# A hybrid SSD and attention encoder layer: z and most of the values projected with tokens on partitions, in blocks of 256 channels

## The chip, the cores and the metric

The kernel runs on one core of one Trainium2 chip. The metric is the device time of one execution in microseconds; the number given for a kernel is the median of its runs. Engines are called as in the profile: TensorE (PE, its weight loads PEld), VectorE (DVE), ScalarE (ACT), GpSimd (POOL) and SyncE (SP), whose queue issues every DMA of this kernel.

## What is computed

One encoder layer on a sequence of 1024 tokens of width 1024, in float32. The cut below leaves out the details of the two halves.

```
h   = layer_norm(x)
z, xbc, dt_f, dt_b, q, k, v, g = split(h @ w_in)       # 1024, 1536, 16, 16, 1024 x 4 channels
y_ssm  = rms_norm(ssd(conv_silu(xbc), dt_f, dt_b) * silu(z))   # forward and backward, chunks of 128
y_attn = rms_norm((softmax1 - lam * softmax2) @ v) * silu(g)   # 8 heads, v of 128 channels each
out = layer_norm(alpha * h + concat(y_ssm, y_attn) @ w_out)
```

The gate needs silu(z) with tokens on partitions, since y_ssm is kept so. The weighted sums need v with tokens (the keys) on partitions, since they are the contracted dimension. q, k, g and the convolution's inputs are used with channels on partitions.

## The kernel before, in words

**Precision.** Matrix operands are split in two parts of a reduced float32 (fp32r): a rounded part "hi" and the rest "lo". A product takes three matmuls: hi by hi, lo by hi, hi by lo.

**Projection.** The normalised input lies transposed in SBUF, channels on partitions, as 16 tiles of 128x512 each for hi and lo (`h_hi`, `h_lo`, lines 279 and 280). `Block` (line 296) is a projection of 128 output channels. The lane `fill` (line 328) computes a block in two halves of the sequence: for each half one PSUM bank, 8 steps over the input channels, three matmuls each, with the weights as the stationary operand (128x128) and 512 tokens as the moving one. That is 48 matmuls a block, and there are NB = 52 blocks. When a half is done, the block's `evac` takes the bank.

The lane `weights` (line 306) loads the weights of the next block in two parts of 256 KB into two staging tiles `wst`, and `split_w` splits each part: ScalarE rounds it into `whi`, POOL subtracts to get `wlo`. There are four places each for `whi` and `wlo`; a block of 128 channels uses two.

**z and v before.** Because a block comes out with channels on partitions, z (line 465) and v (line 921) are turned: `evac` copies the bank into an SBUF tile (`zr` or `vc`), and a lane of its own (`z_tail`, `v_tail`) transposes it in four matmuls against the identity into another bank, from where ScalarE takes silu (z) or ScalarE and VectorE split it (v). z goes to DRAM (`zd`) and is read back by the lane `gate` (line 820).

**Order of the blocks.** b, c and x of the first SSD group; z of group 0 (4 blocks); x, b and c of group 1; z of group 1 (4 blocks); then q, k, v, g for each of the 8 heads. A block may have a condition (`when`); q and k of head h, for instance, wait for the scores of head h-2, and v for its weighted sums, because two heads share the tiles in turn (`free_since`, line 883).

**Order of the instructions.** The work is written as lanes (generators), and the class `Loom` (line 47) weaves them into one order: it estimates from a table of costs when each tile will be ready and lets the lane with the lowest rank go on that would not make TensorE wait. The ranks and margins are in `LANES` (line 29); projection (`fill`) has rank 9, so it fills what the others leave. TensorE keeps this order; ScalarE, VectorE, POOL and the DMA queue are ordered by the framework's scheduler.

**Stages in time.** Up to about 105 us: input, norm, first blocks. 105 to 206 us: SSD of group 0 beside the z blocks. 206 to 289: x, b, c of group 1. 289 to 432: SSD of group 1 beside z of group 1 and q, k, v of head 0. From 432: attention, where each head has scores, exponentials, the difference of the two maps (`combine`), transposes of the map and weighted sums of the values (`values`, line 1029, 24 matmuls of 256 columns for 256 queries). From about 960 the output projection joins. Nearly every instruction is recorded with line 140, the line of the helper that issues it, so the rows are told apart by their tiles: `bk<-hh,whi` is a projection's hi by hi, `bk<-ident,zr` a transpose of z, `bk<-wh,vh` a weighted sum.

Of the kernel before, what the change touches and what calls it, by code (L numbers as in the profile page):

```python
# [18 lines left out]
S = 1024  # L19
# [3 lines left out]
NB = 52  # L23
# [4 lines left out]
# rank of each lane, and how much later than estimated it takes its inputs to be ready  # L28
# [101 lines left out]
class Engine:  # L130
    """An engine whose instructions are noted in the loom."""
# [21 lines left out]
class Pool:  # L153
    """A tile pool whose slots' reuse is noted in the loom; under are the pools whose place it takes."""
# [62 lines left out]
def hybrid_layer_kernel(  # L217
# [70 lines left out]
    def places_w():  # L288
        return [wp.tile([128, 4, 128], F32R, name=n, bufs=4) for n in ("whi", "wlo")]
# [6 lines left out]
    class Block:  # L296
        """128 projected channels; evac(half, psum) takes each half of the sequence."""

        def __init__(self, col, evac, when=None, after=None):
            self.col, self.evac, self.when, self.after = col, evac, when, after  # L300
            self.w, self.begun = [], 0
# [4 lines left out]
    def weights():  # L306
        """Loads and splits the weights of a block while the one before it is computed."""
        for n in range(NB):
# [5 lines left out]
            yield lambda: before.begun > 0  # L314
            sts = []
            for i in range(2):
                st, src = stage_w(b.col, i, wp, 2)
                yield st
                dma(st, src)
                sts.append(st)  # L320
            if not before.pair:
                yield lambda: before.begun > 1
            for st in sts:
                hi, lo = places_w()
                yield (st, hi)
                b.w.append(split_w(st, hi, lo))

    def fill():
        n = 0
        while n < NB:  # L330
# [5 lines left out]
            for b in blocks:  # L336
                if b.when is not None:
                    yield b.when
            for half in range(2):
                for b in blocks:  # L340
# [3 lines left out]
                    for k in range(KB):  # L344
# [10 lines left out]
                        if k == 0:  # L355
                            b.begun += 1
                        if b.last:
# [10 lines left out]
    # ================= embedding LayerNorm and bidirectional SSD =================  # L368
# [30 lines left out]
    def conv_block(b, when, dst_of, after):  # L399
        """Block b of x/B/C: raw projection, then convolution and SiLU into dst_of()."""  # L400
# [31 lines left out]
    def to_tokens(src, put):  # L432
        """Transposes src [128 ch, S]; put(half, psum [128 tokens, 4, 128])."""
# [31 lines left out]
    def z_block(g, j, when=None):  # L465
        def evac(half, ps):
            zr = late["sq"].tile([128, 512], F32, name="zr", bufs=2)
            A.copy(zr, ps)

            def tail():  # L470
                pt = bank((128, 4, 128))
                yield (zr, pt)
                for i in range(4):
                    transpose(pt[:, i, :], zr[:, 128 * i:128 * i + 128])
                zs = late["sq"].tile([128, 4, 128], F32, name="zs", tag="zr", bufs=2)
                A.activation(zs, pt, AF.Silu)
                dma(zd[g][4 * half:4 * half + 4, :, 128 * j:128 * j + 128].rearrange("c p n -> p c n"), zs)
                G[g].z_done += 1
            loom.add(tail(), "z_tail")
        queue.append(Block(Z0 + 512 * g + 128 * j, evac, when))  # L480

    with tc.tile_pool(name="dp", bufs=1) as dp_, tc.tile_pool(name="p0", bufs=1) as p0_:
# [45 lines left out]
        def to_channels():  # L528
            for half in range(2):
                for kk in range(0, KB, 4):  # L530
                    pts = [sbank() for _ in range(4)]
                    for js in ((0, 1, 2), (3,)):
                        for k in range(kk, kk + 4):
# [17 lines left out]
                            if half == 0 and k in (1, 3):  # L551
                                b = first[k // 2]
                                b[0].w.append(split_w(b[1], *places_w(), act=AO))
# [22 lines left out]
        def steps_lane():  # L576
            """Step sizes, decays and their sums within chunks."""
# [103 lines left out]
        for b, st in first[:2]:  # L681
            b.w.append(split_w(st, *places_w(), act=AO))
# [12 lines left out]
    def ssd(g):  # L695
# [72 lines left out]
        def maps():  # L768
            """Within-chunk maps of one head, four chunks at a time."""
# [84 lines left out]
    for j in range(4):  # L854
# [5 lines left out]
    for j in range(4):  # L860
# [453 lines left out]
```

## Time and profile before

| | us |
|---|---|
| median of 3 runs | 1239.81 |
| the runs | 1235.19 to 1240.91 |
| span of the profiled execution (its own time is not given otherwise) | 1236.1 |
| TensorE busy | 1176.0 (95%) |
| VectorE busy | 933.8 (76%) |
| ScalarE busy | 677.8 (55%) |
| POOL busy | 479.9 (39%) |

The span runs from the first to the last instruction of the profiled execution and is that execution's time as far as it is recorded. Busy time counts an instruction from start to end; matmuls overlap, so the sum of their durations is larger than the time they take, and the distance from one start to the next is what one costs. A row of the timeline gives start, duration, engine, line, operation, tiles and shape.

### The profile page before, as it was taken

How to read it: one execution, taken by the hardware profiler on the slowest of the kernel's cores; microseconds unless marked ns; L12 is line 12 of the kernel's file. 1: busy time of each engine (PE TensorE's matmuls, PEld its weight loads, DVE VectorE, ACT ScalarE, POOL GpSimd, SP SyncE). 2: the span in 40 equal slices, each digit the busy share in tenths (PEclk: the TensorE clock that was granted, in tenths of full speed). 3: DMA queues.
4: the chain of work that ended last, by engine and by line, in shares of the span. 5: the costliest groups of instructions: out<-in, count | busy, mean ns of one | idle time of the engine just before them, and what ended most of it. 6: DMA issues, size and time to landing. Idle time of an engine off the chain costs nothing. (4 is left out here: it accounts for less than half of the span.)

```text
span 1236.1 us, 16398 instructions
## 1 busy us (share of the span) xinstructions
PE 1176.0 (95%) x5881; PEld 922.4 (75%) x5881; DVE 933.8 (76%) x1334; ACT 677.8 (55%) x1181; POOL 479.9 (39%) x404
## 2 busy tenths in 40 slices
PE   5998999899899999999999999999999998999997
PEld 3787666788567777777787777877777776778885
DVE  6687888867988568788788787887878889962334
ACT  4556356734457456665755656556656687641221
POOL 7422664323654323223332333233332429541354
PEclk9999999999899999999999999999999998999999
DMA  6113335522245421012112111121111263233221
GB/s 198 32 33 112 89 112 167 178 69 65 89 118 151 132 72 49 26 44 51 26 35 52 43 44 35 34 52 35 43 28 47 81 209 107 55 123 112 78 85 60
DMA packets 107591, 98.03 MB, mean 79 GB/s; under 512 B 9364, under 2 KB 79349, under 8 KB 107509
## 3 DMA queue, kind: packets, MB, share of 16 engines
q1 hardware_dynamic: 107509, 96.98, 27.2%
q8 instruction: 46, 0.75, 0.2%
q14 instruction: 36, 0.29, 0.1%
HBM read 75.85 MB, written 16.91 MB: 75 GB/s over the span
## 5 line engine op out<-in xcount | busy, mean ns | idle before, releaser
L140 PE MATMUL bk<-hh,whi 128*128 128x512 f32 x832 | 353.2, 425 | 0.6
L140 PE MATMUL bk<-hl,whi 128*128 128x512 f32 x832 | 327.0, 393 | 3.2 <-POOL hl L140 2.8
L140 PE MATMUL bk<-hh,wlo 128*128 128x512 f32 x832 | 328.0, 394 | 0.0
L140 ACT ACTIVATE p<-p,nm 128x1024 f32<-128x1024 f32 x128 | 146.8, 1148 | 121.7 <-DVE nm L140 121.0
L140 POOL TENSOR_TENSOR wlo<-wst,whi 128x512 fp32r<-128x512 f32 x104 | 161.5, 1557 | 126.9 <-ACT whi L140 109.2
L140 POOL TENSOR_SCALAR p<-p,rs 128x1024 f32<-128x1024 f32 x56 | 64.5, 1152 | 350.4 <-DVE rs L140 287.5
L140 PEld LDWEIGHTS bk<-hh,wlo 128*128 128x128 f32 x832 | 156.6, 188 | 34.9
L140 PEld LDWEIGHTS bk<-hl,whi 128*128 128x128 f32 x832 | 157.7, 190 | 32.9 <-POOL hl L140 5.4
L140 PEld LDWEIGHTS bk<-hh,whi 128*128 128x128 f32 x832 | 157.7, 190 | 32.7 <-issue 5.8
L140 DVE CUSTOM_DVE_ANT_0 p<-sc,dist 128x1024 f32<-128x1024 f32 x128 | 151.3, 1218 | 11.6 <-PE sc L140 10.9
L140 DVE SCALAR_TENSOR_TENSOR p<-p,rs,p 128x1024 f32<-128x1024 f32 x64 | 128.4, 2007 | 22.1 <-POOL p L140 18.0
L140 DVE TENSOR_TENSOR wl<-bk,wh 128x512 fp32r<-128x512 f32 x128 | 87.0, 684 | 15.6 <-ACT wh L140 13.7
L140 ACT CAST wh<-bk 128x512 fp32r<-128x512 f32 x128 | 74.1, 580 | 43.2 <-PE bk L140 42.7
L140 ACT CAST whi<-wst 128x512 fp32r<-128x512 f32 x104 | 64.2, 620 | 46.9 <-PE bk L140 38.1
L140 PE MATMUL bk<-ident,p 128*128 128x128 f32 x512 | 79.4, 278 | 4.7 <-DVE wl L140 2.7
L140 PEld LDWEIGHTS bk<-ident,p 128*128 128x128 f32 x512 | 61.6, 142 | 29.5 <-DVE wl L140 6.2
L140 PE MATMUL bk<-wh,vh 128*128 128x256 f32 x256 | 74.6, 291 | 0.0
L140 PE MATMUL bk<-wl,vh 128*128 128x256 f32 x256 | 72.2, 282 | 0.7 <-DVE wl L140 0.7
L140 PE MATMUL sc<-kk,q 128*128 128x512 f32 x256 | 72.3, 393 | 0.0
L140 PE MATMUL bk<-wh,vl 128*128 128x256 f32 x256 | 72.0, 281 | 0.0
L140 ACT ACT_TABLE_LOAD x42 | 53.9, 1283 | 25.5 <-DVE t L140 15.7
L140 PEld LDWEIGHTS bk<-xt,t 128*128 128x128 f32 x256 | 45.8, 192 | 26.5 <-issue 15.0
(217 smaller groups left out, 2188.1 us busy)
## 6 DMA issues: line engine op xcount, KB each, us to landing
wst<-in_w_in_dram SPq DMA_DIRECT2D x104, 256.0 KB, 3.0
t<-acs_d SPq DMA_DIRECT2D x64, 256.0 KB, 3.5
ws<-in_w_out_dram SPq DMA_DIRECT2D x32, 256.0 KB, 3.1
ys<-yd SPq DMA_DIRECT2D x32, 256.0 KB, 3.0
xb<-in_x_dram SPq DMA_DIRECT2D x8, 512.0 KB, 6.2
zd<-zs SPq DMA_DIRECT2D x16, 256.0 KB, 2.5
gz<-zd SPq DMA_DIRECT2D x16, 256.0 KB, 3.3
yd<-ys SPq DMA_DIRECT2D x16, 256.0 KB, 2.8
```

The costliest lines, as they stand in the source:

```text
L140: r = f(*args, **kw)
```

## The change

z and the values of heads 1 to 6 are projected the other way round: a tile of the normalised input (128 tokens) is the stationary operand and the weights of 256 channels are the moving one, so that the result has tokens on partitions. `fill_wide` computes such a block as four PSUM banks, each with two groups of 128 tokens by 256 channels; a group is 8 steps of three matmuls with 256 columns, a block 192 matmuls. z takes 4 such blocks instead of 8, and the values of heads 1 and 2, 3 and 4, 5 and 6 take one each; NB falls from 52 to 45. Heads 0 and 7 keep the old way. silu of z and the split of v read the projection's banks directly.

A wide block's weights come in four parts of 256 input rows by 256 channels, of the same 256 KB, through the same two staging tiles, and use all four places of `whi` and `wlo`. `weights` now waits, before it takes a place, until the block that had it has been computed from it (`spent`), and it loads part i+2 after the split of part i.

The values have three places in turn instead of two (head modulo 3): place 0 in the pool `ep`, 1 and 2 in the pool `ap`, so v waits for the sums of the head three before. The wide block of heads h and h+1 waits for head h-2. The places of the third pair of value tiles are among those that the output projection's rows take later (`late_rows`). The descriptor scratch of the DMAs is set to 1024 bytes. Comments and docstrings are gone too.

```diff
-NB = 52
+NB = 45
...
-    def stage_w(col, i, pool, bufs):
-        st = pool.tile([128, 4, 128], F32, name="wst", bufs=bufs)
-        return st, w_in[512 * i:512 * i + 512, col:col + 128].rearrange("(k p) n -> p k n", p=128)
+    def stage_w(col, i, pool, bufs, n=1):
+
+        st = pool.tile([128, 4 // n, 128 * n], F32, name="wst", bufs=bufs)
+        r = 512 // n
+        return st, w_in[r * i:r * i + r, col:col + 128 * n].rearrange("(k p) c -> p k c", p=128)
...
+    def places_w(b):
+        placed.append((b, len([1 for a, _ in placed if a is b])))
+        n = b.wide
+        return [wp.tile([128, 4 // n, 128 * n], F32R, name=t, bufs=4) for t in ("whi", "wlo")]
...
+            parts = 2 * b.wide
             sts = []
...
+            for i in range(parts + 2):
+                if i >= 2:
+                    if i == 2 and not before.pair:
+                        yield lambda: before.begun > 1
+                    a, j = placed[-4] if len(placed) > 3 else (b, -1)
+                    yield lambda: a.spent > j
+                    hi, lo = places_w(b)
+                    yield (sts[i - 2], hi)
+                    b.w.append(split_w(sts[i - 2], hi, lo))
+                if i < parts:
+                    st, src = stage_w(b.col, i, wp, 2, b.wide)
+                    yield st
+                    dma(st, src)
+                    sts.append(st)
+
+    def fill_wide(b):
+        for i in range(4):
+            ps = bank((128, 2, 256))
+            loom.held.add(ps.name)
+            half = i // 2
+            yield ps
+            for t in range(2):
+                c = 128 * (2 * i + t - 4 * half)
+                c = slice(c, c + 128)
+                for k in range(KB):
+                    if len(b.w) <= k // 2:
+                        yield lambda: len(b.w) > k // 2
+                    hi, lo = b.w[k // 2]
+                    yield (hi, lo)
+                    hi, lo = hi[:, k % 2, :], lo[:, k % 2, :]
+                    T.matmul(ps[:, t, :], h_hi[half][k][:, c], hi, start=(k == 0), stop=False)
+                    T.matmul(ps[:, t, :], h_lo[half][k][:, c], hi, start=False, stop=False)
+                    T.matmul(ps[:, t, :], h_hi[half][k][:, c], lo, start=False, stop=(k == KB - 1))
+                    if k == 0 and i % 2 == 0 and t == 0:
+                        b.begun += 1
+                    if i == 3 and t == 1:
+                        b.spent = (k + 1) // 2
+            b.evac(i, ps)
+            loom.held.remove(ps.name)
...
     def z_block(g, j, when=None):
-        def evac(half, ps):
-            zr = late["sq"].tile([128, 512], F32, name="zr", bufs=2)
-            A.copy(zr, ps)
...
-        queue.append(Block(Z0 + 512 * g + 128 * j, evac, when))
+        def evac(i, ps):
+            zs = late["sq"].tile([128, 2, 256], F32, name="zs", tag="zr", bufs=2)
+            A.activation(zs, ps, AF.Silu)
+            dma(zd[g][2 * i:2 * i + 2, :, 256 * j:256 * j + 256].rearrange("c p n -> p c n"), zs)
+            G[g].z_done += 1
+        queue.append(Block(Z0 + 512 * g + 256 * j, evac, when, wide=True))
...
+    def places_v(h):
+
+        H = heads_[h]
+        pool = att["ap"] if h % 3 else ep
+        H.vh, H.vl = [pool.tile([128, NCH, 128], F32R, name=f"{n}{h % 3}") for n in ("vh", "vl")]
+
+    def proj_vv(h):
...
+            for n, H in enumerate(pair):
+                if i == 0:
+                    places_v(h + n)
+                t, c = slice(2 * i, 2 * i + 2), slice(128 * n, 128 * n + 128)
+                A.copy(H.vh[:, t, :], ps[:, :, c])
+                V.tensor_sub(H.vl[:, t, :], ps[:, :, c], H.vh[:, t, :].bitcast(F32))
+                H.v += 0.5
+        free = (lambda: state["open"]) if h == 1 else (lambda: heads_[h - 2].summed == 4)
+        queue.append(Block(V0 + 128 * h, evac, free, wide=True))
...
-        queue.append(Block(V0 + 128 * h, evac, free_since(h, "summed", 4)))
+        queue.append(Block(V0 + 128 * h, evac, None if h == 0 else lambda: heads_[h - 3].summed == 4))
...
+                ("vh2", (2, 512), 1, lambda: heads_[5].summed == 4), ("vl2", (2, 512), 1, None),
                 ("gate", (2, 512), 2, lambda: heads_[6].done == 2),
...
-    nc = _bacc.Bacc("TRN2", target_bir_lowering=False, num_devices=1)
+    nc = _bacc.Bacc("TRN2", target_bir_lowering=False, num_devices=1,
+                     dynamic_dma_scratch_size=1024)
```

## Rows read from the trace of the kernel before

**Rows 1.** Busy time by stretch: length, then busy us (count) per engine.

```profile
core 0: us, PE busy (x) PEld busy (x) DVE busy (x) ACT busy (x) POOL busy (x), PEclk, DMA share, GB/s
105.00:206.00 101.00, 93.63 (x430) 68.13 (x430) 83.97 (x108) 57.29 (x111) 53.04 (x42) 0.98 0.34 103
289.00:432.00 143.00, 131.87 (x615) 99.53 (x614) 113.68 (x150) 71.17 (x136) 67.57 (x54) 0.98 0.40 116
480.00:960.00 480.00, 478.13 (x2581) 378.32 (x2580) 388.46 (x579) 293.14 (x511) 147.39 (x108) 1.00 0.16 40
960.00:1110.00 150.00, 140.48 (x712) 111.48 (x711) 125.55 (x172) 103.89 (x174) 77.91 (x53) 0.97 0.37 116
1110.00:1236.00 126.00, 118.27 (x510) 95.55 (x509) 44.99 (x83) 22.71 (x34) 49.61 (x41) 0.98 0.27 84
```

**Rows 2.** Waits of TensorE: total us, times, longest.

```profile
PE sb L140 <- DVE H L140: 9.1, 8, 2.7
PE bk L140 <- DVE t L140: 5.9, 5, 1.5
...
PE bk L140 <- ACT vc L140: 1.5, 2, 1.0
...
PE bk L140 <- ACT zr L140: 1.0, 1, 1.0
```

**Rows 3.** TensorE's timeline: projection, then the first set of a v block.

```profile
493.81 0.39 PE L140 MATMUL bk<-hh,whi 128*128 128x512 f32 x1
...
497.69 0.39 PE L140 MATMUL bk<-hh,wlo 128*128 128x512 f32 x1
498.20 0.65 PE L140 MATMUL bk<-ident,vc 128*128 128x128 f32 x4
498.61 0.48 PE L140 MATMUL bk<-hh,whi 128*128 128x512 f32 x1
498.93 0.39 PE L140 MATMUL bk<-hl,whi 128*128 128x512 f32 x1
```

**Rows 4.** TensorE's timeline: a second set of v, and a set of z.

```profile
588.28 0.63 PE L140 MATMUL bk<-ident,vc 128*128 128x128 f32 x4
588.67 0.48 PE L140 MATMUL bk<-hh,whi 128*128 128x512 f32 x1
588.98 0.39 PE L140 MATMUL bk<-hl,whi 128*128 128x512 f32 x1
...
363.78 0.60 PE L140 MATMUL bk<-ident,zr 128*128 128x128 f32 x4
364.21 0.33 PE L140 MATMUL bk<-xt,t 128*128 128x64 f32 x2
```

**Rows 5.** Timeline: 24 matmuls of a weighted sum, and one weight load.

```profile
700.90 0.28 PE L140 MATMUL bk<-wh,vh 128*128 128x256 f32 x1
...
703.66 0.28 PE L140 MATMUL bk<-wh,vl 128*128 128x256 f32 x1
...
701.02 0.19 PEld L140 LDWEIGHTS bk<-wh,vl 128*128 128x128 f32 x1
```

**Rows 6.** Tiles zr, whi, wlo (ns min/median/max), and DMA issues (KB, us to landing).

```profile
L140 ACT COPY zr<-bk x16: 562/578/590, 118.7 to 390.2; 128x512 f32<-128x512 f32 x16
...
L140 ACT CAST whi<-wst x36: 600/618/639, 109.2 to 430.0; 128x512 fp32r<-128x512 f32 x36
L140 POOL TENSOR_TENSOR wlo<-wst,whi x36: 1267/1306/2351, 109.9 to 430.6; 128x512 fp32r<-128x512 f32 x36
...
L140 POOL TENSOR_TENSOR wlo<-wst,whi x48: 1274/1468/2290, 486.7 to 946.4; 128x512 fp32r<-128x512 f32 x48
...
wst<-in_w_in_dram SPq DMA_DIRECT2D x104, 256.0 KB, 3.0
...
ws<-in_w_out_dram SPq DMA_DIRECT2D x32, 256.0 KB, 3.1
```

**Rows 7.** One third of the projection's matmuls, 480 to 960 us and 105 to 432.

```profile
L140 PE MATMUL bk<-hh,whi 128*128 128x512 f32 x384 | 160.5, 418 | 0.6
...
L140 PE MATMUL bk<-hh,whi x278: 387/393/1414, 105.0 to 429.3; 128*128 128x512 f32 x139
```

**Rows 8.** Waits of SP's queue: total us, times, longest.

```profile
SPq L140 <- POOL wlo L140: 517.0, 95, 29.0
```

**Rows 9.** Busy time of two stretches; the granted clock stands third from the end.

```profile
120.00:160.00 40.00, 36.61 (x175) 27.00 (x174) 33.82 (x44) 18.01 (x35) 22.73 (x18) 0.96 0.29 86
...
320.00:360.00 40.00, 37.69 (x152) 26.07 (x150) 34.08 (x42) 20.82 (x42) 21.22 (x16) 0.91 0.36 101
```

More of the change, by code (lines that the diff above doesn't have):

```diff
@@ L282, in hybrid_layer_kernel @@
     h_used = [0, 0]
-    def stage_w(col, i, pool, bufs):
-        st = pool.tile([128, 4, 128], F32, name="wst", bufs=bufs)
-        return st, w_in[512 * i:512 * i + 512, col:col + 128].rearrange("(k p) n -> p k n", p=128)
-    def places_w():
-        return [wp.tile([128, 4, 128], F32R, name=n, bufs=4) for n in ("whi", "wlo")]
+    def stage_w(col, i, pool, bufs, n=1):
+        st = pool.tile([128, 4 // n, 128 * n], F32, name="wst", bufs=bufs)
+        r = 512 // n
+        return st, w_in[r * i:r * i + r, col:col + 128 * n].rearrange("(k p) c -> p k c", p=128)
+    placed = []
+    def places_w(b):
+        placed.append((b, len([1 for a, _ in placed if a is b])))
+        n = b.wide
+        return [wp.tile([128, 4 // n, 128 * n], F32R, name=t, bufs=4) for t in ("whi", "wlo")]
     def split_w(st, hi, lo, act=A):
@@ L296, in hybrid_layer_kernel, with __init__ @@
     class Block:
-        def __init__(self, col, evac, when=None, after=None):
+        def __init__(self, col, evac, when=None, after=None, wide=False):
             self.col, self.evac, self.when, self.after = col, evac, when, after
-            self.w, self.begun = [], 0
+            self.w, self.begun, self.spent = [], 0, 0
+            self.wide = 2 if wide else 1
             self.pair = self.last = False
@@ L306, in weights @@
     def weights():
-        for n in range(NB):
+        n = -1
+        while n < NB - 1:
+            n += 1
             yield lambda: len(queue) > n
@@ L314, in weights @@
             yield lambda: before.begun > 0
+            parts = 2 * b.wide
             sts = []
[L316 to L326, printed above, removed]
+            for i in range(parts + 2):
[36 more added lines that the diff above has]
+            loom.held.remove(ps.name)
     def fill():
@@ L338, in fill @@
                     yield b.when
+            if blocks[0].wide == 2:
+                yield from fill_wide(blocks[0])
+                continue
             for half in range(2):
@@ L356, in fill @@
                             b.begun += 1
+                        if half:
+                            b.spent = (k + 1) // 4
                         if b.last:
@@ L465, in z_block @@
     def z_block(g, j, when=None):
-        def evac(half, ps):
-            zr = late["sq"].tile([128, 512], F32, name="zr", bufs=2)
-            A.copy(zr, ps)
[L470 to L479, printed above, removed]
-        queue.append(Block(Z0 + 512 * g + 128 * j, evac, when))
+        def evac(i, ps):
[4 more added lines that the diff above has]
+        queue.append(Block(Z0 + 512 * g + 256 * j, evac, when, wide=True))
     with tc.tile_pool(name="dp", bufs=1) as dp_, tc.tile_pool(name="p0", bufs=1) as p0_:
@@ L681, in hybrid_layer_kernel @@
         for b, st in first[:2]:
-            b.w.append(split_w(st, *places_w(), act=AO))
+            b.w.append(split_w(st, *places_w(b), act=AO))
         first = first[2:]
@@ L852, in ssd @@
             loom.add(lane())
-    for j in range(4):
+    for j in range(2):
         z_block(0, j)
@@ L859, in hybrid_layer_kernel @@
     bc_block(1, "c", lambda: G[0].fwd == NCH)
-    for j in range(4):
+    for j in range(2):
         z_block(1, j)
@@ L919, in proj_k, with evac @@
         queue.append(Block(K0 + 128 * h, evac, free_since(h, "scored", 8)))
+    def places_v(h):
[3 more added lines that the diff above has]
+    def proj_vv(h):
+        pair = heads_[h:h + 2]
+        def evac(i, ps):
+            for n, H in enumerate(pair):
[7 more added lines that the diff above has]
+        queue.append(Block(V0 + 128 * h, evac, free, wide=True))
     def proj_v(h):
@@ L925, in evac @@
             if half == 0:
-                H.vh = H.pool().tile([128, NCH, 128], F32R, name="vh")
-                H.vl = H.pool().tile([128, NCH, 128], F32R, name="vl")
+                places_v(h)
             vc = (att["ap"] if h else late["sq"]).tile([128, 512], F32, name="vc", tag="zr", bufs=2)
@@ L956, in project_head @@
     def project_head(h):
-        for f in (proj_q, proj_k, proj_v, proj_g):
+        if h % 2 == 0 or h == 7:
+            fs = (proj_q, proj_k, proj_v, proj_g) if h in (0, 7) else (proj_q, proj_k, proj_g)
+        else:
+            fs = (proj_q, proj_k, proj_vv, proj_g)
+        for f in fs:
             f(h)
```

2 lines of the change are left out of this document (1 added, 1 removed), and 2 rows, old and new, of the table last.

## The prediction

> **What bounds the kernel now.** I read the busy time by stretch first, since the page's average mixes stages. In the attention stretch, 480 to 960 us, TensorE is busy for 478.1 of 480 us, VectorE for 388 and ScalarE for 293 [rows 1]: there every microsecond of TensorE time taken away should come off the end, and every hole put in should be added. In the two SSD stretches (105 to 206 and 289 to 432 us) TensorE is busy for 93.6 of 101 and 131.9 of 143, and VectorE for 83 and 79% of the time. Two things share the limit there: projection work, which fills the gaps, and a chain through VectorE. From 960 us on TensorE again does nearly all (140.5 of 150, 118.3 of 126). The waits of TensorE come next: little stands there at all, and most of it is the SSD's (9.1 us for the state tile H, 5.9 for the maps t), against 1.0 us for the z copies and 1.5 for the v copies [rows 2]. So I price TensorE's time first, by the distance from start to start in its timeline, because the printed durations overlap.
>
> **What goes: 112 transposes.** z loses 16 sets of four, heads 1 to 6 lose 12 sets; heads 0 and 7 keep theirs.
> A v block has two sets. Around the first, the last projection matmul starts at 497.69 and the transposes at 498.20, though a matmul takes 0.228 us to the next start (17 steps from 493.81 to 497.69) [rows 3]: 0.28 us of waiting for the copy out of PSUM. The four then hold the engine until 498.61, and the first matmul behind them takes 0.32 instead of 0.23. Start of the next regular matmul: 498.93, where without the set it would have been 498.15. The set costs 0.78 us. The second set waits for nothing: from 588.28 to 588.98, less one matmul, 0.47 us [rows 4]. Six blocks by 1.25 us: -7.5 us.
> A z set takes 0.43 us (363.78 to 364.21) and is followed by other small work, so no slow restart comes on top [rows 4]. 16 by 0.43 is 6.9 us; the wait for the copies adds 1.0 [rows 2]: -7.9 us.
>
> **What comes: twice as many matmuls of half the width.** 7 wide blocks of 192 matmuls with 256 moving columns (1344) stand in for 14 blocks of 48 with 512 (672). The same form already runs in the weighted sums of the values: 128x128 stationary, 256 columns, a fresh weight load each, 23 steps from 700.90 to 703.66 us, 0.120 us per step [rows 5]. 1344 x 0.120 = 161.3 us. The old form: 672 x 0.228 = 153.4; I take 154 since short runs elsewhere step by 0.23. So +7 us (+6 to +8), of which 3/7 in the attention stretch. Each form carries 13 to 15 ns beyond its columns at the granted full clock of 2.4 GHz, and halving the width pays that twice.
> The Trainium skill (TensorE: Matmul & The Clock Gate, section "Back-to-back issue gap") gives N/2.4 + 2.5 ns for an isolated matmul, with a fixed cost of only 2.5 ns. By that two narrow ones would cost 2.5 ns more than one wide one, 1.7 us over 672 instead of 7, and the sum would be 5 us better; the rows differ from it, and I go by them.
> Net on TensorE: -7.5 - 7.9 + 7 = -8.4 us.
>
> **ScalarE, VectorE, POOL.** 28 copies out of PSUM of 0.58 us leave ScalarE [rows 6]; SiLU of z and the splits of v stay, now straight from the projection's banks. In the attention stretch ScalarE is 61% busy, so this is worth nothing by itself; in the SSD stretches, where it feeds the chain, it may be worth something: 0 to -6 us, a third of the 18.5 us in which TensorE idles there [rows 1]. I take 0, because the waits on record name VectorE's tiles. The weight splits are as many as before (104 on ScalarE, 104 on POOL).
>
> **DMA.** The loads of weights are as many and as large (38 x 2 + 7 x 4 = 104 of 256 KB), with rows of 1 KB instead of 512 B for the wide ones. Loads of the same size with rows of 2 KB (w_out) land after 3.1 us, those of 512 B after 3.0 [rows 6]: no gain. The stores of z keep number and size. No DMA here is issued by POOL, so I cost the smaller scratch at 0: it frees SBUF for the third place of values. That place costs nothing and loosens one wait: v of heads 3 and 4 wait for head 1's sums, as v of head 3 did before.
>
> **The new wait: places for weights.** A wide block holds all four places of split weights until its last 128 tokens. The next block's first split can begin only when the first quarter of the last 24 matmuls is done, 18 x 0.120 = 2.2 us before the block's end. Cast 0.62 us on ScalarE, subtraction 1.3 to 1.5 on POOL [rows 6]: ready about at the end. Before, splits were done a block ahead.
> Wide to narrow (5 times): part 0 in time to some tenths late, part 1 done 1.1 us after the end and needed 12 x 0.228 = 2.7 after. Narrow to wide (5 times): the fourth part's place comes free with the narrow block's last matmul and its split takes 1.9 us; it is needed after 18 x 0.120 = 2.2. So 0 to 1 us each, by how long ScalarE and POOL have other work in front. Wide to wide (twice, between the z blocks): there are two staging tiles, so the load of part 2 waits for POOL's subtraction of part 0, takes 3.0 us, and its split 1.9: ready 4.7 us after the end, needed after 1.4; part 3 0.6 later still. About 4 to 4.5 us of bare projection time each.
> Bare sum: 9 for the two, up to 10 for the ten others. What covers it: projection is only 55% of the attention stretch (3 x 384 matmuls by 0.228 are 263 of 480 us) and 58% of the time from 105 to 432 us (3 x 278, 190 of 327 us) [rows 7], so the last 24 matmuls and the first of the next block are spread over twice the time, and the planner puts other lanes where weights are late. If the cover is gone, the 19 us count in full. Bounds 0 and +19; I take +3, near the lower end, as the trace shows two lanes side by side in every stretch in question. Behind the waiting casts stand the exponentials of the scores on ScalarE, behind the waiting loads the k shifts and decay rows on SP's queue. That queue already stands for 517 us in all behind POOL's subtraction [rows 8] while TensorE hardly waits for anything it brings, so I add nothing.
>
> **The sum.** -8.4 + 3 = -5.4 us: 1236.1 (the profiled span; no other time of that execution is recorded) to 1230.7. The span is 3.7 us under the median of 1239.8 and inside the runs shown (1235.2 to 1240.9), so I predict 1234.4 for the median. 0.5% is 6.2 us, about what a measurement of this kernel can tell from no change: faster means under 1233.6.
>
> **Rivals.**
> *The SSD's share is lost.* If VectorE's chain sets the end of the SSD stretches, z's transposes cost nothing today and their removal brings nothing; then only -7.5 + 3 in attention counts, with 2 us of holes: about 1237.3. For it: VectorE at 80% there, H as the longest wait. Against: TensorE at 92%, and work left over is done later anyway.
> *More than the transposes goes.* If every hand-over is covered and the chain runs freer without z copies and ring waits on ScalarE: -8.4 - 6, 1225.4. For it: 18.5 us of idle TensorE in these stretches. Against: only 1.0 us of it is put down to z.
> *Slower: weights come late.* The mechanism above, uncovered: -8.4 + 19 = +10.6, 1250.4. It decides from 8.4 us of holes on (slower at all), 14.6 for a clear loss. The place is between the two z blocks of each group, and at each wide block's ends. The clock may add to it: in the stretches 120 to 160 and 320 to 360 us, just where these blocks fall, the granted clock was 0.96 and 0.91 [rows 9], so part of them ran at the lower level of 1.2 GHz after idle patches; 9% of 40 us is 3.6 us of work lost in the second, and longer holes could cost that again.
> *The narrow form doesn't reach its pitch.* If a matmul had to wait for its own load of 0.19 us [rows 5], 1344 x 0.07 us would be 94 us more, about 1330. The rows that price it show loads of 0.19 us overlapping at 0.120 us per step, so 1%.
>
> **Chances.** Forecast 44%: holes of 0 to 6 us put it between -8.4 and -2.4, a third of it past the bound of -6.2 (16% faster, 28% the same). SSD's share lost 16%: nearly all the same. More goes 25%: nearly all faster. Late weights 14%: 11% slower, 3% the same. Pitch 1%. Together faster 0.40, same 0.46, slower 0.14. The range 1224 to 1247 leaves out the far end of the good case and the worse half of the late weights. The likeliest case alone spans 1231 to 1238.
>
> **What would show it.** Right: distances of 0.12 us between the new matmuls; no transposes of zr, and four sets of vc; the period of an attention head shorter by about 0.7 us on average, odd heads long and even ones short; holes of under 2 us at the hand-overs. Wrong: TensorE idle before the first matmuls of a wide block's successor, released by POOL's subtraction; low clock around 155 and 335 us for longer than now; a steeper pitch; or the SSD's end staying at 432 us while its TensorE time falls.

## The result, and the profile after

The changed kernel takes **1271.87 us** (median of 4 runs, 1264.21 to 1277.12), the kernel before, timed with it, 1240.36: a ratio of **1.0258**, 95% interval 1.0222 to 1.0294. It is slower by 2.6%, where 1234.4 us was predicted with a range of 1224 to 1247. The profiled execution is the shortest of the four; its span grew from 1236.1 to 1262.5 us, +26.4, and these are the microseconds that the traces can place. The other 5 of the median's 31.5 are seen only in that the mean granted clock of the four runs is 0.972 to 0.985, against 0.990 in the trace of before.

Busy time by stretch, kernel after (length, then busy us and count for each engine, granted clock, DMA share, GB/s), to be laid beside [rows 1]:

```profile
105.00:206.00 101.00, 85.84 (x538) 69.01 (x537) 87.00 (x111) 52.92 (x104) 50.39 (x39) 0.98 0.33 103
289.00:432.00 143.00, 133.42 (x789) 109.34 (x788) 110.09 (x155) 69.33 (x129) 66.47 (x53) 0.98 0.39 114
480.00:960.00 480.00, 463.65 (x2732) 382.55 (x2731) 356.66 (x566) 281.31 (x495) 141.66 (x106) 0.99 0.16 39
960.00:1110.00 150.00, 132.51 (x690) 103.82 (x689) 125.86 (x185) 100.24 (x170) 67.04 (x47) 0.97 0.31 95
1110.00:1262.00 152.00, 143.34 (x639) 116.53 (x638) 59.49 (x101) 36.88 (x59) 60.98 (x49) 0.99 0.30 93
```

TensorE's idle time (length less busy) went from 7.4 to 15.2 us in the first SSD stretch, from 11.1 to 9.6 in the second, from 1.9 to 16.3 in attention and from 9.5 to 17.5 in the stretch where the output projection joins. What ended the waits of TensorE, kernel after (total us, times, longest):

```profile
PE sb L140 <- DVE H L140: 15.2, 10, 3.7
...
PE bk L140 <- DVE osl L140: 8.9, 4, 2.7
...
PE bk L140 <- DVE wl L140: 3.6, 4, 2.2
...
PE bk L140 <- DVE vl L140: 2.3, 1, 2.3
```

Against [rows 2], H has grown by 6 us, and osl, wl and vl now stand there with 14.8. POOL's `wlo`, the late weights that the prediction feared, is not in this list. The list names only what ended a wait, though; whether projection work stood ready to fill it has to be looked up for each hole. The longest hole of attention in TensorE's timeline, kernel after:

```profile
687.64 0.28 PE L140 MATMUL bk<-whi,hh 128*128 128x256 f32 x1
...
688.96 0.28 PE L140 MATMUL bk<-wlo,hh 128*128 128x256 f32 x1
689.08 0.60 PE L140 MATMUL bk<-ident,p 128*128 128x128 f32 x4
689.91 0.49 PE L140 MATMUL bk<-osh,ones_r 128*128 128x512 f32 x1 [0.23 <-ACT osh L140]
693.10 0.51 PE L140 MATMUL bk<-osl,ones_r 128*128 128x512 f32 x1 [2.69 <-DVE osl L140]
693.44 0.40 PE L140 MATMUL bk<-hh,whi 128*128 128x512 f32 x1
```

The same time on VectorE, then on POOL:

```profile
689.09 2.28 DVE L140 SCALAR_TENSOR_TENSOR p<-p,rs,p 128x1024 f32<-128x1024 f32 x1
691.29 1.75 DVE L140 TENSOR_TENSOR osl<-osq,osh 128x512 fp32r<-128x512 f32 x1
```

```profile
690.24 2.25 POOL L140 TENSOR_TENSOR wlo<-wst,whi 128x512 fp32r<-128x512 f32 x1
```

From 687.64 to 688.96 the wide form takes 11 steps of 0.120 us, the price that was taken from [rows 5]. Then TensorE stops at a matmul of the lane `finish` (the sum of squares that closes a part of a head, `ones_r`), which the planner had put first and whose operand `osl` VectorE makes only after a difference of two maps of 2.28 us. But the projection's next block was not ready either: the low part of its first weights is done at 692.49 us, 3.2 us after the wide block's end. The hole from 859.00 to 861.68 us has the same two causes. In the other holes of attention over 0.4 us, 10.3 of the 16.3 us, the weights of the next projection matmul stood ready. This one lies within a group of a wide block:

```profile
820.88 0.28 PE L140 MATMUL bk<-wlo,hh 128*128 128x256 f32 x1
821.00 0.60 PE L140 MATMUL bk<-ident,p 128*128 128x128 f32 x4
823.85 0.47 PE L140 MATMUL bk<-osh,ones_r 128*128 128x512 f32 x1 [2.24 <-DVE wl L140]
...
824.38 0.40 PE L140 MATMUL bk<-whi,hh 128*128 128x256 f32 x1
```

```profile
812.08 1.29 POOL L140 TENSOR_TENSOR wlo<-wst,whi 128x512 fp32r<-128x512 f32 x1 [0.32 <-ACT whi L140]
```

The weights for 824.38 were split by 813.37 us, and the group's bank was open. TensorE keeps the planner's order, so a matmul placed too early stops everything behind it.

How far attention moved is read from the first score matmul of each head. Of the eight in the kernel after (duration in ns, start in us), three:

```profile
L140 PE MATMUL sc<-kk,q x1: 477/477/477, 435.1 to 435.1; 128*128 128x512 f32 x1
...
L140 PE MATMUL sc<-kk,q x1: 390/390/390, 516.4 to 516.4; 128*128 128x512 f32 x1
...
L140 PE MATMUL sc<-kk,q x1: 393/393/393, 1015.6 to 1015.6; 128*128 128x512 f32 x1
```

The heads start at 435.1, 516.4, 599.9, 675.6, 767.4, 844.2, 936.1 and 1015.6 us. Before, they start at 432.4, 509.6, 589.4, 669.2, 749.1, 828.8, 908.6 and 989.1: a cycle that repeats to 0.2 us for five heads. This splits the 26.4 us without a rest: attention begins 2.7 later, the first head takes 81.3 instead of 77.2 (+4.1), the next six together 499.2 instead of 479.5 (+19.7), and from the last head's start to the end of the span it is 246.9 instead of 247.0.

### The profile page after: what moved, and what is told of

It reads as the page before. It is cut to its first block, busy times and chain, and to the rows that moved or that the text cites. A ratio compares the mean times of both kernels' runs of the same rounds, so it can differ in the third digit from the quotient of the medians.

```text
span 1262.5 us, 17501 instructions
## 1 busy us (share of the span) xinstructions
PE 1173.2 (93%) x6441; PEld 952.7 (75%) x6441; DVE 903.8 (72%) x1346; ACT 668.0 (53%) x1166; POOL 473.1 (37%) x404
## 5 line engine op out<-in xcount | busy, mean ns | idle before, releaser
L140 PE MATMUL bk<-hh,whi 128*128 128x512 f32 x608 | 250.0, 411 | 2.5 <-ACT raw L140 2.1
L140 PE MATMUL bk<-hl,whi 128*128 128x512 f32 x608 | 239.7, 394 | 3.2 <-POOL hl L140 3.0
L140 PE MATMUL bk<-hh,wlo 128*128 128x512 f32 x608 | 240.2, 395 | 0.0
L140 PE MATMUL bk<-whi,hh 128*128 128x256 f32 x448 | 145.0, 324 | 0.0
L140 PEld LDWEIGHTS bk<-hh,whi 128*128 128x128 f32 x608 | 114.9, 189 | 28.2 <-issue 3.6
L140 PE MATMUL bk<-whi,hl 128*128 128x256 f32 x448 | 127.1, 284 | 0.0
L140 PE MATMUL bk<-wlo,hh 128*128 128x256 f32 x448 | 127.1, 284 | 0.0
L140 DVE TENSOR_TENSOR wl<-bk,wh 128x512 fp32r<-128x512 f32 x128 | 87.4, 685 | 26.4 <-ACT wh L140 24.5
L140 PEld LDWEIGHTS bk<-whi,hh 128*128 128x128 f32 x448 | 86.3, 193 | 5.7 <-issue 5.1
L140 PEld LDWEIGHTS bk<-whi,hl 128*128 128x128 f32 x448 | 86.4, 193 | 5.5 <-issue 5.1
L140 PEld LDWEIGHTS bk<-wlo,hh 128*128 128x128 f32 x448 | 85.9, 192 | 0.2 <-POOL wlo L140 0.2
L140 PEld LDWEIGHTS bk<-ident,p 128*128 128x128 f32 x512 | 60.2, 141 | 34.0 <-issue 14.2
```

The costliest lines, as they stand in the source:

```text
L140: r = f(*args, **kw)
```

## The experiments

Sixteen further kernels. **Margin** below is a number of the planner's table `LANES`: microseconds that it adds to the time at which it expects a lane's tiles to be ready. It changes no operand, no size and no count of an instruction, only the order. The **end of the plan** is the planner's own sum of estimated costs in its bookkeeping, no time of the chip. In the table, "ratio" is to the kernel before on the same chip (medians of runs on different chips are not compared, only what each has over that), "first" the start of head 0's scores, "cycle" the mean distance of the starts of heads 1 to 7, "rest" from head 7's start to the end of the span (us, profiled execution).

| kernel | median | ratio (95%) | span | first | cycle | rest |
|---|---|---|---|---|---|---|
| before | 1240.4 | 1 | 1236.1 | 432.4 | 79.9 | 247.0 |
| after | 1271.9 | 1.0258 (1.0222–1.0294) | 1262.5 | 435.1 | 83.2 | 246.9 |
| e1 z wide | 1282.2 | 1.0323 (1.0280–1.0365) | 1286.0 | 444.8 | 87.1 | 237.8 |
| e2 values wide | 1263.4 | 1.0187 (1.0157–1.0217) | 1262.0 | 434.5 | 83.9 | 246.1 |
| e3 places, scratch | 1239.3 | 1.0003 (0.9987–1.0020) | 1236.5 | 430.4 | 79.9 | 248.9 |
| e4 after, banks freed early | 1279.3 | 1.0312 (1.0282–1.0342) | 1277.3 | 441.7 | 86.7 | 235.1 |
| e5 after, values 0.2 | 1250.1 | 1.0112 (1.0088–1.0136) | 1248.5 | 442.4 | 82.1 | 233.6 |
| e6 before, values 0.2 | 1246.6 | 1.0090 (1.0067–1.0114) | 1244.0 | 435.3 | 80.3 | 251.8 |
| e7 before, values 0.8 | 1284.6 | 1.0400 (1.0374–1.0425) | 1282.3 | 431.3 | 88.4 | 237.5 |
| e8 after, values 0.2, 5 places | 1254.3 | 1.0149 (1.0115–1.0184) | 1250.6 | 440.2 | 82.3 | 239.4 |
| e9 after, values 0.3 | 1251.0 | 1.0113 (1.0085–1.0141) | 1247.1 | 436.7 | 80.6 | 246.7 |
| e10 z wide, scores 1.2 | 1254.3 | 1.0135 (1.0110–1.0161) | 1249.1 | 439.1 | 80.4 | 246.5 |
| e11 after, finish 2.2, 5 places | 1253.2 | 1.0121 (1.0098–1.0144) | 1246.6 | 436.4 | 80.7 | 249.3 |
| e12 before, combine 0.4 | 1241.9 | 1.0033 (1.0018–1.0048) | 1240.3 | 432.9 | 80.1 | 249.1 |
| e13 values wide, values 0.2 | 1249.3 | 1.0089 (1.0068–1.0111) | 1246.7 | 432.8 | 83.7 | 233.3 |
| e14 values wide, finish 2.2 | 1260.1 | 1.0180 (1.0159–1.0201) | 1259.3 | 437.5 | 83.8 | 241.9 |
| e15 z wide, group 0 only | 1246.2 | 1.0056 (1.0036–1.0075) | 1244.5 | 439.8 | 79.9 | 248.2 |
| e16 z wide, group 1 only, scores 1.2 | 1245.1 | 1.0054 (1.0037–1.0072) | 1246.9 | 436.1 | 80.5 | 246.7 |

### The parts alone, and the banks: e1 to e4

e1 keeps the wide z, e2 the wide values, e3 neither (three places for values and the small scratch alone). e4 is the changed kernel with wide values copied out of their bank at once.

```diff
e1, NB = 48:
-        if h % 2 == 0 or h == 7:
-            fs = (proj_q, proj_k, proj_v, proj_g) if h in (0, 7) else (proj_q, proj_k, proj_g)
-        else:
-            fs = (proj_q, proj_k, proj_vv, proj_g)
-        for f in fs:
+        for f in (proj_q, proj_k, proj_v, proj_g):
... (v of heads 1 and 2 waits for state["open"], since no head stands three before them)
e2: z_block and its calls as before, NB = 49
e3: both, NB = 52
e4:
+                if n == 0:
+                    vc = att["ap"].tile([128, 2, 256], F32, name="vc", tag="zr", bufs=2)
+                    A.copy(vc, ps)
-                A.copy(H.vh[:, t, :], ps[:, :, c])
-                V.tensor_sub(H.vl[:, t, :], ps[:, :, c], H.vh[:, t, :].bitcast(F32))
+                A.copy(H.vh[:, t, :], vc[:, :, c])
+                V.tensor_sub(H.vl[:, t, :], vc[:, :, c], H.vh[:, t, :].bitcast(F32))
```

> z wide, all values narrow with three places. Theory BANKS (the wide blocks of values hold the four shared PSUM banks until VectorE's subtraction, so projection stalls in attention): the attention stretch is as full as before (TensorE 478 of 480 us), only the holes between the wide z blocks stay, 1240 + 4 = 1244 us (1238 to 1250). Theory WEIGHTS (late split weights at every wide block): 4 of the 7 wide blocks are left, more than half of the loss, 1256 us (1252 to 1262).

> z narrow with transposes, values of heads 1 to 6 wide. BANKS: nearly the whole loss stays, 1263 us (1257 to 1270), with TensorE idle for 12 us or more between 480 and 960 us. WEIGHTS: 3 of 7 wide blocks, 1253 us (1248 to 1257), and the idle time stands right behind the three wide blocks.

> Nothing wide: z and values as before, but three places of values, the places' tags, late rows and small scratch of the change. BANKS and WEIGHTS: 1240 us (1236 to 1244). Rival PLACES (the third place or the scratch itself costs): over 1250 us.

> The change, but a wide block of values is copied out of PSUM by one ScalarE copy per bank and split from SBUF, so the bank is free without VectorE. BANKS: the holes of attention go (TensorE 475 of 480 us or more) and with them part of the thin tail, 1272 - 14 - 6 = 1252 us (1245 to 1257). WEIGHTS: no change, 1272 us (1267 to 1276).

e3 sits on the kernel before: the third place and the scratch cost nothing. e2 came out as the theory BANKS had it, with 16.3 us of idle TensorE between 480 and 960 us. What either theory expected of e1 and e4 fell. z alone loses 3.2%, more than the whole change, and the parts don't add (+3.2 and +1.9 against +2.6). Freeing the banks early made it slower, but e4 got another order as well (its cycle is 86.7 us), so it doesn't clear the banks. The strangest is e1: its attention has the same instructions as the kernel before, yet their cycle went from 79.9 to 87.1 us. Its busy time by stretch, columns as above:

```profile
480.00:960.00 480.00, 467.98 (x2508) 372.70 (x2507) 356.56 (x549) 285.88 (x493) 138.44 (x105) 1.00 0.16 39
960.00:1110.00 150.00, 123.72 (x600) 96.10 (x599) 115.51 (x164) 90.68 (x152) 64.18 (x46) 0.90 0.30 93
```

12 us of idle TensorE where before had 1.9, and 26 in the next stretch instead of 9.5, with the weights of the next projection matmul ready in every hole over 0.4 us up to 960. The likeliest way for a change in the SSD to reach that far is the order that the planner writes. This is the theory of the next runs.

### One margin, and nothing else: e5 to e8

```diff
(one entry of the line LANES; the rest of the line is left out)
e5, after; e6, before; e8, after with bufs=5 for whi, wlo and placed[-5]:
-values=(4.25, 0.4)
+values=(4.25, 0.2)
e7, before:
-values=(4.25, 0.4)
+values=(4.25, 0.8)
```

> The change with one number of the planner altered: the margin of the lane `values` 0.2 instead of 0.4. Theory WEAVE (the wide blocks shift the state in which attention begins and how projection is spread in it, the planner's order falls out of the regular cycle of the kernel before, and the loss is that order's): the attention stretch is full again (TensorE over 474 of 480 us), 1240 us (1234 to 1247). Rival OWN WAITS (late weights and held banks of the wide blocks, which this number doesn't touch): 1262 us or more.

> The kernel before with the same number altered, 0.2 instead of 0.4. Both theories: within 0.5% of the kernel before (1234 to 1246 us), so that the number is no gain by itself.

> The kernel before with the margin of `values` at 0.8: no projection, weight or bank is altered. WEAVE: the regular cycle is lost here too, 1270 us (1258 to 1285), with TensorE idle for 8 us or more between 480 and 960 us and a thin tail. OWN WAITS: nothing of its waits is in this kernel, 1236 to 1246 us.

> The change with `values` at 0.2 and five places for split weights instead of four (a place falls free a quarter of a wide block earlier). If the SSD's holes are late weights, attention begins 5 us earlier than in the run with four places and the whole is 1230 us (1224 to 1236). If they are VectorE's chain alone, no change against that run, 1240 us.

e7 has nothing wide in it and loses 4.0%, more than the change. Its stretches look like those of e1:

```profile
480.00:960.00 480.00, 458.29 (x2413) 364.90 (x2410) 342.51 (x523) 273.75 (x471) 135.82 (x101) 0.98 0.15 39
960.00:1110.00 150.00, 128.93 (x633) 99.36 (x633) 118.24 (x172) 93.81 (x158) 65.23 (x46) 0.91 0.28 88
```

So an order that leaves the cycle is enough for a loss of this size. In the other direction one number takes 17 us off the changed kernel: it had 31.5 us over the kernel before, e5 has 14.2. But e5 missed its mark, 1250.1 where 1247 at most was expected, with TensorE busy for 469.9 of 480 us where over 474 was expected; the rival's 1262 is missed by more. e6 was expected within 0.5% and lost 0.9: a margin has a price of its own, and at this margin on both sides the change costs 3.5 us, 1250.1 against 1246.6. In e8 the fifth place did not help, at 1254.3 after 1250.1, and attention began 2.2 us earlier where 5 was expected; neither 1230 nor 1240 us was reached. That doesn't settle late weights: of the second z block the last two parts were split by 166.6 and 170.9 us in e8 and by 166.9 and 171.3 in e5, hardly earlier; e8 still has two staging tiles.

### Other orders: e9 to e12

```diff
e9, after:   values=(4.25, 0.4) -> 0.3
e10, e1 and: scores=(4, 0.8) -> 1.2
e11, after with five places as in e8, values 0.4: finish=(4.2, 2) -> 2.2
e12, before: combine=(4.125, 0.6) -> 0.4
```

> The changed kernel with the margin of the lane `values` at 0.3 in place of 0.4, and no other edit. At 0.2 the same kernel had 1250.1 us, at 0.4 1271.9, and by the planner's own bookkeeping 0.3 gives the regular order of all that were tried (end of its plan 1104.5, against 1111.0 at 0.2, 1127.8 at 0.4 and 1112.0 for the kernel before). Order theory: nearly all of the loss in attention is the order, so with the regular order the kernel takes what the wide forms take by themselves: 1236 to 1248 us, and the heads' scores start 78 to 82 us apart. Rival, the wide blocks stop TensorE whatever the order: not under 1255, with heads up to 90 us apart.

> The kernel with the wide form for z alone (1282.2 us), and the margin of the lane `scores` at 1.2 in place of 0.8. Nothing in the projection of z or in the SSD differs. Order theory: the 43 us that z alone had lost were some 12 us up to the start of attention (its x attention started at 444.8 us against 432.4) and the rest the order of the lanes in attention; with a regular order only the 12 stay: 1245 to 1256 us. Rival, the wide z costs the 43 us itself: not under 1272.

> The changed kernel with five places for the weights' parts and the margin of the lane `finish` at 2.2 in place of 2 (the `values` margin back at 0.4). Order theory: 1238 to 1250 us, as its plan is short (1099.0) and the order regular; the extra place alone had not helped (1254.3 us at a margin of 0.2). Rival, margins and places don't matter, the wide banks do: 1262 or more.

> The kernel before with the margin of the lane `combine` at 0.4 in place of 0.6, nothing wide. By the planner's bookkeeping its plan is as short as before's own (1108.1 against 1112.0). Order theory: a margin costs nothing where the order stays regular: 1230 to 1243 us. Rival, any departure from the tuned margins costs some per cent: 1250 or more, as 0.8 for `values` cost 4%.

e10 is the clearest: the wide z untouched, one margin moved, 3.2% of loss down to 1.35, as the order theory said. Its stretches:

```profile
105.00:206.00 101.00, 87.39 (x527) 71.23 (x526) 79.50 (x108) 52.18 (x101) 51.58 (x39) 0.93 0.33 101
...
480.00:960.00 480.00, 478.56 (x2596) 383.04 (x2595) 374.96 (x580) 297.36 (x512) 145.59 (x109) 1.00 0.16 41
```

From 480 to 960 us TensorE is as full as before (478.6 of 480). Of the span's +13.0 us 6.7 lie ahead of attention, where the SSD is, and 6.8 between the starts of head 0 and head 7, most of it in the first distance (81.1 for 77.2) and the last (84.6 for 80.5). e12 came out near the top of its range. e9 and e11 missed theirs by 3 us each, and the rivals' 1255 and 1262 were not reached either: the cycle came back to 80.6 and 80.7, but not all of the time with it. So 19 of the 31.5 us go with the order (e9 has 12.5 over the kernel before); 12 to 18 us stay in each of the other orders tried with z wide (e5, e8 to e11). Part of what stays is the margin's own price: at 0.2 for `values`, 10.7 of e5's 14.2 us are there without the change (e6). For the other margins moved with wide forms no such pair was run. In e9 all the idle time of TensorE from 480 to 960 us is of one kind, once behind each wide block of values:

```profile
PE bk L140 <- DVE vl L140: 6.6, 3, 2.3
```

These 6.6 us are 1.1 for each of six heads, most of what separates e9's 80.6 us from the 79.2 that the prediction's 0.7 less would have given. The first of the three, on VectorE and then on TensorE:

```profile
535.23 1.75 DVE L140 TENSOR_TENSOR osl<-osq,osh 128x512 fp32r<-128x512 f32 x1
...
536.90 0.41 DVE L140 TENSOR_TENSOR vl<-bk,vh 128x256 fp32r<-128x256 f32 x1
```

```profile
537.45 0.47 PE L140 MATMUL bk<-osh,ones_r 128*128 128x512 f32 x1 [2.26 <-DVE vl L140]
537.76 0.39 PE L140 MATMUL bk<-osl,ones_r 128*128 128x512 f32 x1
```

The matmul that stops TensorE doesn't read `vl`; it waits for the bank that VectorE empties with it. But the next one reads `osl`, which is made only by 536.98 us, so the held bank accounts for half a microsecond at most and the rest is once more a `finish` ahead of its operand.

### What stays: e13 to e16

```diff
e13, e2 and: values=(4.25, 0.4) -> 0.2
e14, e2 and: finish=(4.2, 2) -> 2.2
e15, e1 and (z_block_narrow is the z_block of before):
-    for j in range(2):
-        z_block(1, j)
+    for j in range(4):
+        z_block_narrow(1, j)
e16, e1 and the same for z_block(0, j), and: scores=(4, 0.8) -> 1.2
```

> The kernel with wide values alone (1263.4 us, z narrow as before), and the margin of the lane `values` at 0.2 in place of 0.4; the end of its plan falls from 1127.9 to 1108.8. Theory, the left-over sits in z's wide blocks in the SSD: the wide values then cost nothing in a regular order, 1232 to 1245 us, with first scores at 430 to 436 us. Rival, it sits in the values (banks of two heads held, holes at the ones that close a head): 1248 or more.

> The kernel with wide values alone, and the margin of the lane `finish` at 2.2 in place of 2, `values` back at 0.4; end of the plan 1111.1. The same question by another margin, since one margin has its own cost (0.9% for `values` at 0.2 in the kernel before). Theory, left-over in z: 1232 to 1245 us. Rival, in the values: 1248 or more.

> z wide for the first group of heads alone (the two wide blocks at 105 to 216 us), narrow for the second; values narrow; all margins as in the kernel before. End of the plan 1112.1, as before's 1112.0. Theory, the first stretch of the SSD carries z's loss (5 to 6 us more idle and a lower clock at 105 to 206 us): first scores at 436 to 441 us instead of 432, and 1243 to 1252 us in all. Rival, the second stretch carries it: first scores by 433, 1234 to 1241.

> z wide for the second group alone (two wide blocks at about 295 to 400 us), narrow for the first; values narrow; the margin of the lane `scores` at 1.2 in place of 0.8, as in the run of z alone that fell to 1254 us; end of the plan 1107.3. Theory, the first stretch carries z's loss: first scores at 428 to 434 us, 1234 to 1244 us in all. Rival, the second stretch carries it: first scores from 436, 1246 or more.

e15 is the run to read, because the planner's cycle in attention is the one of before (79.8 to 79.9 us for each head). With it nearly the whole difference lies ahead of attention: first scores at 439.8 instead of 432.4, +7.4 of the span's +8.4, though half of z's transposes are gone. Against e3, which has the same places and nothing wide, it is +9.4 of +8.0. Two pieces of the first SSD stretch, kernel before and then e15, columns as above:

```profile
160.00:180.00 20.00, 19.80 (x86) 13.63 (x85) 16.49 (x23) 10.27 (x17) 13.45 (x11) 1.00 0.38 106
180.00:206.00 26.00, 24.99 (x116) 17.56 (x115) 23.35 (x34) 18.35 (x38) 13.14 (x10) 1.00 0.46 147
```

```profile
160.00:180.00 20.00, 15.38 (x85) 11.84 (x83) 17.05 (x23) 6.85 (x14) 12.51 (x10) 0.91 0.43 125
180.00:206.00 26.00, 23.64 (x122) 17.48 (x121) 22.63 (x33) 16.00 (x34) 11.76 (x10) 0.87 0.41 131
```

TensorE idles 5.8 us more in these 46 us and works at a granted clock of 0.91 and 0.87 instead of 1.00, so a part of it at 1.2 GHz instead of 2.4. The idle patch ahead of it, in e15's timeline, is a wait for the state tile a few matmuls into the second wide block of z. Here it is with the last matmul of the first block, and then POOL's splits of the second block's last three parts of weights:

```profile
157.25 0.28 PE L140 MATMUL bk<-wlo,hh 128*128 128x256 f32 x1
...
164.05 1.12 PE L140 MATMUL sb<-H,c_ch 128*128 128x512 f32 x2 [3.43 <-DVE H L140]
```

```profile
158.35 1.72 POOL L140 TENSOR_TENSOR wlo<-wst,whi 128x512 fp32r<-128x512 f32 x1
...
164.71 1.72 POOL L140 TENSOR_TENSOR wlo<-wst,whi 128x512 fp32r<-128x512 f32 x1
...
169.07 1.72 POOL L140 TENSOR_TENSOR wlo<-wst,whi 128x512 fp32r<-128x512 f32 x1
```

The first block ends at 157.5 us; the third and fourth part of the second are ready at 166.4 and 170.8, 8.9 and 13.3 us later. In the hole only the second part stood ready in full, six matmuls or 0.7 us of work, so projection, in the order of its own steps, could not have filled the 3.43 us. A hole of 3.4 to 3.7 us stands at this place in all nine kernels with z of the first group wide, and none over 2.6 us in the nine others.

e16 starts its scores at 436.1 us, +3.7, as the rival had it (the theory had 434 at most), and its 1245.1 us lie between the two. Not all of this is the second stretch: from 105 to 206 us, with nothing wide there, it already idles 9.0 us, 1.6 more than before. e13 and e14 went against the theory: with the values alone wide no order tried had a cycle under 83.7 us, and 1249.3 and 1260.1 us are the rival's. But e13 stands beside e6, which has the same margin and nothing wide: 1.0089 and 1.0090. At this margin the wide values cost nothing, and with z wide as well (e5, 1.0112) it is 0.2% more. e14's plan was as short as before's, 1111.1, and the kernel took 1260.1 us: the end of the plan doesn't tell the time of the chip.

## Why the prediction was wrong

**Right: the mechanical terms.** z's transposes are gone, four sets of v's are left, and the wide form runs at its 0.120 us. (The Trainium skill, TensorE: Matmul & The Clock Gate, section "Back-to-back issue gap", has 2.5 ns beyond the columns of an isolated matmul, which for 256 columns gives an estimate of 0.109 us; the 0.120 us of this trace differ from it, as those of the one before did.) `vc` is copied 4 times, `zr` no more. The copies, the weights' splits and the loads, kernel after, to be laid beside [rows 6]:

```profile
L140 ACT COPY vc<-bk x4: 578/587/596, 426.5 to 1012.4; 128x512 f32<-128x512 f32 x4
...
L140 POOL TENSOR_TENSOR wlo<-wst,whi x48: 1279/1295/2280, 483.7 to 955.0; 128x512 fp32r<-128x512 f32 x48
...
wst<-in_w_in_dram SPq DMA_DIRECT2D x104, 256.0 KB, 3.0
```

The loads, 28 of them now with rows of 1 KB, land in 3.0 us as before, and e3 confirms the zero for places and scratch. TensorE's busy time in all fell from 1176.0 to 1173.2 us at a mean clock of 0.985 instead of 0.990. The sum of -8.4 is not tested better than that: busy time times clock gives 4.7 us less for e7 than for the kernel before, at the same work.

**Mis-sized: the new wait.** The weights do come late, and later than the prediction had it. Between the two z blocks of the first group it had the third and fourth part ready 4.7 and 5.3 us after the first block's end; they came 8.9 and 13.3 us after it in e15, 9.9 and 14.3 in the kernel after. Wide to narrow it had "some tenths late"; it was 3.2 and 3.3 us behind two of the three blocks of values, in the two longest holes of attention. The prediction gave other work in front 0 to 1 us; POOL's rows show more (in e15, between two splits, it decays H and then waits 1.96 us for VectorE before its next product). The profile hides this, because the waits are put down to `H` and `osl`: in the page's groups of weight loads `wlo` releases 0.2 and 0.3 us. What the late weights cost by themselves is not known. No run took them away: e8 left the two staging tiles, and a run with more of them was not made. The rival "Slower: weights come late" has the right sign and a part of the cause; 10.3 us of idle time in attention had weights ready, and e1 and e7 lose more with no wide block in attention at all.

**Wrong: the step "What covers it".** It said that the planner puts other lanes where weights are late, and took that for cover. So it put the new order that the planner then writes at nothing, without a reason. This is the step that failed. Before, the blocks of a head and its lanes repeat every 79.9 us. With the change they follow another order, in which matmuls that close a part of a head come before their operands are ready: the waits put down to osl, wl and vl make 13.9 of the 16.3 us in which TensorE idles from 480 to 960 us. Six heads take 19.7 us more, where 0.7 less for each was expected. That the order does most of this, and not the wide matmuls, is what e5, e7, e9 and e10 show, with one number moved each: 17 and 19 of the 31.5 us go in e5 and e9, and e7 loses 4% with nothing wide. Which of the change's parts pushed it out of its cycle was not found, since the wide z and the wide values each do. A rival "the heads leave their cycle" is missing, and its price stood to be had: e7 shows 4% for one number of the planner's table, with no change of work.

**Wrong: "The SSD's share is lost".** It counted z's -7.9 as lost at worst. e15 loses 7.4 us net with half of z wide and the attention cycle unchanged. The step that failed there is the cover again. The holes came where the prediction looked for them, between the two z blocks, and the clock fell in e15 as it feared from [rows 9]; but they end with `H` (waits of 9.1 us before, 15.2 in the kernel after) while next to no projection work is ready. What H and the late weights each cost stays open: in e15 POOL had done its step on H at 161.5 us and VectorE added to it only at 163.3, after a step of the maps, a copy and a product, and no run tried that by itself. Open, too, is whether some order would let the change win. None of those tried beats the kernel before; at the one margin timed with and without the change (`values` 0.2) it costs 3.5 us instead of the 5.4 that it was to save.

## What to carry to other kernels

Where one engine follows an order that a planner wrote from estimates, look first for a cycle in the trace (the start of each head): a change of block size is priced by whether that cycle survives, and only then by its matmuls. Before crediting a saving of half a per cent there, move one margin of the planner in the old kernel and time it; here that alone gave from +0.3 to +4.0%. For each long wait look up whether the work that should have filled it was ready; the releaser in the profile doesn't say. And compare an old and a new form at several margins each: 31.5 and 12.5 us over the kernel before are the same change.

## What was not expected of the hardware

VectorE's differences of two maps took less time in the slower kernel, with the same work, 64 times 128x1024. The group in the page of before, then in the page of after (busy us, mean ns, idle before):

```profile
L140 DVE SCALAR_TENSOR_TENSOR p<-p,rs,p 128x1024 f32<-128x1024 f32 x64 | 128.4, 2007 | 22.1 <-POOL p L140 18.0
```

```profile
L140 DVE SCALAR_TENSOR_TENSOR p<-p,rs,p 128x1024 f32<-128x1024 f32 x64 | 109.0, 1703 | 22.4 <-POOL p L140 17.8
```

VectorE's busy time fell by 30 us in all (933.8 to 903.8) and nothing was gained by it. What goes with the time of a difference is POOL's work: those with no POOL instruction beside them took 1.27 to 1.29 us in both kernels (16 of 64 before, 30 after), those with more than 1 us of POOL's work beside them 2.3 us in the median (46 and 28). So here a busy time fell as POOL's work stood beside it less often. Likewise POOL's subtraction for the weights takes 1.28 us at the least and 2.28 at the most from 480 to 960 us of the kernel after.

The granted clock fell after short idle patches: in the 26 us after 180 us TensorE was 91% busy in e15, at 0.87, and 96% busy before, at 1.00. But it isn't read from busy time alone: from 105 to 120 us it was 0.89 in e15 and 1.00 before, with 12.14 and 12.23 us busy of 15. Nor is this patch the wide form's doing: e3, with nothing wide, had 0.89 there with 12.43 us busy, the kernel after 1.00 with 11.92. The rows of before, e15, e3 and after:

```profile
105.00:120.00 15.00, 12.23 (x58) 9.94 (x58) 10.31 (x10) 10.67 (x23) 3.72 (x4) 1.00 0.24 71
105.00:120.00 15.00, 12.14 (x73) 11.20 (x72) 10.51 (x10) 10.08 (x22) 3.71 (x4) 0.89 0.26 71
105.00:120.00 15.00, 12.43 (x52) 10.20 (x51) 9.60 (x10) 10.66 (x23) 3.69 (x4) 0.89 0.24 71
105.00:120.00 15.00, 11.92 (x85) 10.93 (x84) 10.28 (x10) 10.68 (x23) 3.71 (x4) 1.00 0.27 71
```
